# An SSD branch projection as seven block products, with the sums of its weights made early and the gates kept as tanh

## The chip, the cores and the metric

One Trainium2 chip, one NeuronCore of it. The metric is device time in microseconds (us) for one execution of the kernel; where several runs are given, the median counts. A core has TensorE (PE, matmuls; PEld is its weight load), VectorE (DVE), ScalarE (ACT), GpSimd (POOL) and SyncE (SP, which issues the DMAs), each with an instruction queue of its own that it works through in order.

## The reference

One layer on 1024 tokens of width 1024 in float32: a mixer with two branches, attention (A) and a Mamba-2 state space branch (B, "SSD"), then a gated feed-forward part. The part that matters here is how the branches are merged:

```python
D_MODEL, SEQ, D_INNER = 1024, 1024, 2048
h = rmsnorm(x, pre_norm_mix) * (1.0 + scale_m) + shift_m
q_lat, kv_lat, k_idx, w_idx, z, xbc, dt_raw, g_a, g_b = jnp.split(h @ w_in, IN_SPLITS, axis=-1)
y_a = sparse_mla_attention(...) @ w_o_attn
y_b = ssd_mixer(...) @ w_o_ssd          # rmsnorm(y * silu(z), ssd_norm), 1024 x 2048, times 2048 x 1024
mix = (jax.nn.sigmoid(g_a) * y_a + jax.nn.sigmoid(g_b) * y_b) @ w_out
x = x + gate_m * rmsnorm(mix, post_norm_mix)
h2 = rmsnorm(x, pre_norm_ffn) * (1.0 + scale_f) + shift_f
u_gate, u_up = jnp.split(h2 @ w_ffn_in, 2, axis=-1)
x = x + gate_f * rmsnorm((jax.nn.silu(u_gate) * u_up) @ w_ffn_out, post_norm_ffn)
```

## The kernel before

Activations are held transposed, features on the 128 partitions and tokens along the free dimension, in two halves b = 0, 1 of 512 tokens (`half(b)`). A float32 product is made of three matmuls: both operands are split into a rounded high part and the remainder, and hi x hi, lo x hi and hi x lo are added up in PSUM. One matmul is 128 x 128 weights by 128 x 512 activations. So a product over 16 k-tiles takes 48 matmuls for each tile of 128 outputs and each half.

Weights come as a stream, `W` (class `Stream`, L135): for each 4 k-tiles SP loads `wraw` (256 KB), ACT rounds it to `whi` (L153), POOL subtracts to get `wlo` (L154). The load, the rounding and the subtraction of a tile are issued up to two tiles ahead of the tile in use. Since every queue is in order, `whi` and `wlo` stand behind whatever ACT and POOL were given before. Tile buffers come from arenas: EV for short-lived tiles of 512 columns, `H_`, `Q` and `R` for operands. PSUM has three banks "d" (`bank_d`) and five general ones (`bank`), which the norms use too. A scheduler orders the engines' instructions, except that in the stages marked `in_order` TensorE keeps the order of the code.

The stages that the change touches, in order of time:

- Input projection with the convolved tiles (`conv_group`, L1018) and the gate tiles (`gate`, L970): `conv_group(0)` and `conv_group(1)` come among the first; from group 2 on each tile is followed by one unit of `weight_sums` (L1004), which adds blocks of w_ffn_out on POOL and stores the sums for the feed-forward part, which is computed by seven block products already. Gate a is stored raw in `d_sga`, gate b in `d_gb`.
- The SSD loop, with `beside()` as filler between its steps: the rest of gate b (`gate_run`), the attention branch times w_o_attn (`poa_run`, L1272: a `poa` product, emptied by a DVE copy, stored in `d_ya`), and the first y tiles (`y_load`, L1226: load from `d_y`, ACT scales and rounds to `yh`, DVE makes the remainder `yw` with one scalar_tensor_tensor). The loop writes y, already gated by silu(z), to `d_y`, and sums its squares in `ysq`.
- `merge(b)` (L1362), for each of 8 output tiles: loads of gate b, `d_ya` and gate a, two Sigmoids on ACT, gate a times y_a on DVE, the `pos` product of 48 matmuls over all of y, then `mrg` = pos times the norm `rys`, times gate b (POOL), plus the other branch, and its two parts `mg`.
- `mixed(b)` (L1399): the `pot` product with w_out, 24 matmuls for each of 8 tiles, and the sum of squares for the norm.
- `residual_steps(b)` (L1427): norm, residual, second norm. `ffn_input(b)` (L1453) makes the input of the feed-forward part.

The order is merge(0), mixed(0), merge(1) with the residual of half 0 among its first tiles, mixed(1), and then the early feed-forward products with the residual of half 1 among them. A norm is `rstd` (matmuls into `p`, `v` on DVE at L265, `r` on POOL at L267) and `rspread` (transposes into `prn`, L273).

## Time and profile before

| what | value |
|---|---|
| runs | 2365.05, 2358.47, 2360.74 us; median 2360.74 |
| profiled execution | span 2362.1 us, no other time of it is listed |
| granted TensorE clock, mean | 0.993 of full speed |
| products and norms from the first `pos` (1435.0 us) to the first feed-forward product (1707.7 us) | 272.7 us |
| `whi` on ACT, `wlo` on POOL, mean of one | 627 ns, 1392 ns |
| table loads on ACT at the Sigmoid of `merge` (L1370) | 1, of 1.28 us |

How to read it: the page gives, for each engine, the time in which it was busy and the groups of instructions that cost most, each with its line, its operands, its count, its busy time, the mean duration of one and the idle time before it with what ended it. The timeline lists single instructions by start and duration in us; the windows give the same busy times for stretches of the span. A matmul's duration runs from its start to the modelled end of its pipeline, so that consecutive matmuls overlap.

### The profile page before, as it was taken

The page shows a single profiled execution, that of the slowest core. Times are in us where ns is not written, and L with a number is a line of the kernel's source. Part 1 is how long each engine was busy: PE and PEld are TensorE (multiplying, and loading weights), DVE is VectorE, ACT ScalarE, POOL GpSimd, SP SyncE. Part 2 cuts the span into 40 slices and gives each one's busy share as a digit, 9 for nine tenths or more (in the row PEclk, how much of TensorE's full clock was granted, in tenths as well). Part 3 has the DMA queues.
Part 4 walks back from the last instruction along what each step waited for, and adds up shares of the span by engine and source line. Part 5 has one row for each costly group of instructions (what it writes and reads, how often), then busy time and mean ns, then how long its engine had stood idle before and what let it go on. Part 6 is the DMA issues. An engine that isn't in the chain of part 4 may idle for free. (4 is left out here: it accounts for less than half of the span.)

```text
span 2362.1 us, 35006 instructions
## 1 busy us (share of the span) xinstructions
PE 2326.5 (98%) x11832; PEld 1907.8 (81%) x11832; DVE 1578.2 (67%) x2994; ACT 1217.9 (52%) x2361; POOL 1168.5 (49%) x911
## 2 busy tenths in 40 slices
PE   8999999999999999999999999999999999999997
PEld 5878888888888888888887787888888788888886
DVE  5467887599676777666677875346476766645775
ACT  4346666576545555555676664454545222235542
POOL 1445552522244555552445455556768545554556
PEclk9999999999999999999999999999999999999999
DMA  7137542623222323334678766566474444428665
GB/s 270 63 134 238 193 169 94 196 90 101 96 81 85 99 90 101 95 94 150 217 245 282 240 220 227 184 209 197 126 265 134 142 152 154 159 95 280 210 190 171
DMA packets 237891, 386.10 MB, mean 163 GB/s; under 512 B 24032, under 2 KB 91792, under 8 KB 237712
## 3 DMA queue, kind: packets, MB, share of 16 engines
q1 hardware_dynamic: 224464, 362.31, 47.1%
q10 hardware_dynamic: 13248, 21.56, 3.1%
q8 instruction: 93, 1.52, 0.3%
q14 instruction: 86, 0.70, 0.1%
HBM read 288.07 MB, written 98.85 MB: 164 GB/s over the span
## 5 line engine op out<-in xcount | busy, mean ns | idle before, releaser
L154 POOL TENSOR_TENSOR wlo<-wraw,whi 128x512 fp32r<-128x512 f32 x246 | 341.7, 1392 | 420.6 <-ACT whi L153 381.4
L1533 PE MATMUL p<-xh,wr 128*128 128x512 f32 x880 | 273.1, 391 | 2.4 <-DVE g L1623 2.4
L153 ACT ACTIVATE whi<-wraw 128x512 fp32r<-128x512 f32 x246 | 153.7, 627 | 207.5 <-issue 58.8
L1527 POOL TENSOR_TENSOR wr<-a,wr 128x512 fp32r<-128x512 f32 x107 | 151.1, 1426 | 95.3 <-ACT wr L1526 63.2
L1533 PEld LDWEIGHTS p<-xh,wr 128*128 128x128 f32 x880 | 166.0, 189 | 37.3 <-DVE g L1623 2.8
L1533 PE MATMUL p<-xl,wr 128*128 128x512 f32 x440 | 171.8, 390 | 0.0
L249 POOL TENSOR_TENSOR fwl<-fw,fwh 128x512 fp32r<-128x512 f32 (+1 forms) x78 | 108.8, 1406 | 102.3 <-ACT fwh L248 38.7
L323 POOL TENSOR_TENSOR adaw<-adaw,cs 128x512 f32<-128x512 f32 x64 | 68.3, 1067 | 156.3 <-DMA adaw<-ada_w 128.0
L853 ACT ACTIVATE lg<-lg,mx 128x256 f32<-128x256 f32 (+7 forms) x128 | 99.0, 774 | 56.5 <-DVE mx L850 56.2
L1526 ACT ACTIVATE wr<-a 128x512 fp32r<-128x512 f32 x107 | 65.9, 629 | 108.4 <-PE p L1533 80.9
L648 DVE SCALAR_TENSOR_TENSOR acc<-rel,widx,acc 128x384 f32<-128x384 f32 (+2 forms) x90 | 104.9, 1190 | 15.4 <-ACT rel L643 15.2
L1533 PE MATMUL p<-h2h,wr 128*128 128x512 f32 x352 | 110.2, 391 | 1.0 <-ACT xh L248 1.0
L698 ACT ACTIVATE junk<-acc,cand__2215 128x1024 bf16<-128x1024 f32 (+2 forms) x96 | 86.2, 898 | 39.4 <-DVE cand__2215 L741 30.6
L228 PE MATMUL pos<-yh,wlo 128*128 128x512 f32 x256 | 101.4, 396 | 1.0 <-POOL wlo L154 1.0
L228 PE MATMUL pos<-yh,whi 128*128 128x512 f32 x256 | 100.7, 393 | 1.3 <-ACT whi L153 1.3
L643 ACT ACTIVATE rel<-prel 128x512 f32<-128x512 f32 (+3 forms) x160 | 77.0, 523 | 46.8 <-PE prel L642 43.3
L228 PE MATMUL pos<-yw,whi 128*128 128x512 f32 x256 | 100.7, 393 | 0.0
L1533 PEld LDWEIGHTS p<-xl,wr 128*128 128x128 f32 x440 | 82.9, 188 | 17.3
L1527 POOL TENSOR_TENSOR wr<-s,wr 128x512 fp32r<-128x512 f32 x44 | 61.7, 1407 | 65.1 <-ACT wr L1526 58.7
L696 DVE TENSOR_SCALAR_CACHE_REDUCE junk<-acc,cand__2224 128x896 bf16<-128x896 f32 (+2 forms) x96 | 88.5, 922 | 1.5
L850 DVE CUSTOM_DVE_ANT_0 lg<-plg,nm 128x256 f32<-128x256 f32 (+1 forms) x128 | 51.5, 403 | 53.0 <-PE plg L841 52.3
L874 PE MATMUL pt<-ident,lg 128*128 128x128 f32 x576 | 82.3, 272 | 0.0
(671 smaller groups left out, 7301.5 us busy)
## 6 DMA issues: line engine op xcount, KB each, us to landing
wraw<-w_in SPq DMA_DIRECT2D x129, 256.0 KB, 2.9
a<-w_ffn_in SPq DMA_DIRECT2D x122, 256.0 KB, 3.3
al<-d_a SPq DMA_DIRECT2D x88, 256.0 KB, 4.5
adaw<-ada_w SPq DMA_DIRECT2D x64, 256.0 KB, 2.9
al<-d_ac SPq DMA_DIRECT2D x32, 512.0 KB, 5.1
wraw<-w_o_ssd SPq DMA_DIRECT2D x64, 256.0 KB, 3.1
d_a<-g SPq DMA_DIRECT2D x42, 256.0 KB, 2.2
ada<-ada_p SPq DMA_DIRECT2D x16, 512.0 KB, 7.8
```

The source lines that it names most:

```text
L153: self.hi = behind(S.activation(hi[:, :kt], raw[:, :kt], AF.Copy))
L154: self.lo = behind(G.tensor_tensor(lo[:, :kt], raw[:, :kt], f(hi[:, :kt]), op=OP.subtract))
L228: T.matmul(o, wt[:, k0 + i, :], xs[k][xi][b][:, sl], start=pi == 0 and i == 0 and wt is hi and xi == 0, stop=pi == len(pcs) - 1 and i == l ...
L249: (lo_eng or V).tensor_tensor(lo, src, f(hi), op=OP.subtract)
L643: S.activation(rel[:, 512 * b:512 * b + w_], pr[:, 0:w_], AF.Relu)
L648: V.scalar_tensor_tensor(acc[i][:, 0:n], rel[:, 0:n], ws, acc[i][:, 0:n], op0=OP.mult, op1=OP.add)
L696: V.tensor_scalar(jk, y, a_, 0.0, op0=op, op1=OP.add, accum_out=o)
L698: S.activation(jk, y, AF.Sign, scale=-1.0, bias=a_, accum_out=o)
L853: S.activation(lg[:, 0:n], lg[:, 0:n], AF.Exp, scale=-1.0, bias=m, accum_out=rr[:, 2 * t + hh:2 * t + hh + 1])
L874: T.transpose(ptv[:, hh, t, :], PR[hh, t][:, j * P:(j + 1) * P], ident)
L1527: G.tensor_tensor(w[:, 1], src, f(w[:, 0]), op=OP.subtract)
L1533: T.matmul(p, w[:, wi, i], X[x][i][xi], start=start and i == 0 and k == 0, stop=i == 3 and k == 2, skip_group_check=True)
```

## The change

The projection by w_o_ssd is cut into blocks: the two halves of the tokens, the first and the last 8 of its 16 k-tiles (SK = 8), and the first and the last four of its 8 output tiles. Seven products of such blocks, each over 8 k-tiles for 4 output tiles c, take the place of the eight that two halves, two k-blocks and two output blocks make. A step (i, c) of `ssd_step` is one product i for one tile c, 24 matmuls; products add up in the same PSUM bank or are added from SBUF. Operands: product 1 is the first 8 k-tiles of half 0 with the weights as they are, 2 the last 8 of half 0; 3, 5, 6 and 7 have sums of y tiles (`last_sum`, `both_sums`, `third_sum`), 4 the last 8 k-tiles of half 1. The weights of 4 to 7 are sums of blocks, from `d_s`. The order is `SEQ` (22 steps), mixed(0), `SEQ1` (6 steps, with the residual of half 0 between them), mixed(1). Each step first gives ACT, DVE and POOL its `tasks`: sums and splits for later steps, and gates; their loads are issued one step before.

The sums of the weights are made by `ssd_sums`, in eight units on POOL with buffers and code like those of `weight_sums`, after the last two tiles of `conv_group(0)`, the four of `conv_group(1)` and the first two z gates. Gates are stored as tanh(x/2), so that a sigmoid is (tanh + 1)/2; the two halves are taken together as a scale of 0.5 where `mix` leaves PSUM. Gate a is multiplied in `poa_run`, with `d_sga` loaded into `ya` there; gate b with the norm in `merge_gate`. The Sigmoids go. Half of the `xr` additions of half 0 move to POOL.

```diff
-    def gate(c, dst, fn):
+    def gate(c, dst, fn, scale=1.0):
         p = wide(c)
         for b in BS:
             t = EV("g")
-            S.activation(t, p[b], fn)
+            S.activation(t, p[b], fn, scale=scale)
...
+    s_units = iter([(c, k0) for c in range(4) for k0 in (0, 4)])
+    def ssd_sums(c, k0):
+        b11, b12, b21, b22 = sum_bufs
+        for x, t, o in ((b11, c, 0), (b12, 4 + c, 0), (b22, 4 + c, SK), (b21, c, SK)):
+            tc.add_manual_dep(SP.dma_start(x, a["w_o_ssd"][t][:, o + k0:o + k0 + 4]).ins, W.issue, mybir.DependencyInfo(
+                mybir.DependencyClass.NoSync, mybir.DependencyReason.DATA), reason="behind")
+        G.tensor_tensor(b11, b12, b11, op=OP.subtract)
+        G.tensor_tensor(b12, b22, b12, op=OP.subtract)
+        G.tensor_tensor(b22, b11, b22, op=OP.subtract)
+        G.tensor_tensor(b21, b21, b22, op=OP.add)
+        for i, x in enumerate((b11, b22, b12, b21)):
+            SP.dma_start(d_s[i, c][:, k0:k0 + 4], x)
     def conv_group(g):
-        for t in group_tiles(g):
+        for i, t in enumerate(group_tiles(g)):
             conv_out(conv(*t))
             if g > 1:
                 weight_sums(*next(units))
+            elif g or i > 1:
+                ssd_sums(*next(s_units))
...
+    def y_raw(k, b):
+        t = EV("yl")
+        SP.dma_start(t, d_y[k][:, half(b)])
+        return t
+    def y_parts(i, j, src, where, scale=None, eng=V):
+        hi, lo = where("yh", dt=F32R), where("yw", dt=F32R)
+        if scale is None:
+            ins = S.activation(hi, src, AF.Copy)
+            eng.tensor_tensor(lo, src, f(hi), op=OP.subtract)
+        else:
+            ins = S.activation(hi, src, AF.Copy, scale=scale)
+            V.scalar_tensor_tensor(lo, src, scale, f(hi), op0=OP.mult, op1=OP.subtract)
+        YO[i][j] = hi, lo
+        return ins.ins
+    def y_load(ks, places):
         for k in ks:
-            t = EV("yl")
-            SP.dma_start(t, d_y[k][:, half(b)])
-            where = places(k)
-            yh, yw = where("yh", dt=F32R), where("yw", dt=F32R)
-            j = S.activation(yh, t, AF.Copy, scale=col("ssd_norm", k))
-            if b == 0 and k > 11:
-                tc.add_manual_dep(j.ins, W.hi, mybir.DependencyInfo(
-                    mybir.DependencyClass.NoSync, mybir.DependencyReason.DATA), reason="behind")
-            V.scalar_tensor_tensor(yw, t, col("ssd_norm", k), f(yh), op0=OP.mult, op1=OP.subtract)
-            YB[b][k] = ([yh] * 2, [yw] * 2)
+            y_parts(1 + k // SK, k % SK, y_raw(k, 0), places(k), col("ssd_norm", k))
...
         def poa_run(t, b, w):
             ya = EV("ya")
+            SP.dma_start(ya, d_sga[t][:, half(b)])
             p = bank_d("poa")
             yield from dense_steps(p, b, w, AT)
-            if t:
-                V.tensor_copy(ya, p)
-            else:
-                anchor(S.activation(ya, p, AF.Copy))
+            i = V.scalar_tensor_tensor(ya, ya, 1.0, p, op0=OP.add, op1=OP.mult)
             SP.dma_start(d_ya[t][:, half(b)], ya)
...
-            S.activation(sb, sb, AF.Sigmoid)
-            S.activation(ga, ga, AF.Sigmoid)
-            V.tensor_tensor(ld, ld, ga, op=OP.mult)
-            p = bank_d("pos")
-            pcs = wpieces(list(range(16))) if t or b else [(first_w, 0, ks8[:4])] + wpieces(list(range(4, 16)))
-            dense([(p, b, ALL)], pcs, YB[b])
...
+    def merge_in(t, b):
+        sb, ld = EV("sgb"), EV("yal")
+        for x, src in ((sb, d_gb), (ld, d_ya)):
+            SP.dma_start(x, src[t][:, half(b)])
+        return sb, ld
+    def merge_gate(b, sb):
+        V.scalar_tensor_tensor(sb, sb, 1.0, rys[b], op0=OP.add, op1=OP.mult)
+    def merge_out(t, b, src, sb, ld, eng=V):
+        V.tensor_tensor(sb, src, sb, op=OP.mult)
+        eng.tensor_tensor(sb, sb, ld, op=OP.add)
+        hi, lo = in_r("mg")
+        i1 = S.activation(hi, sb, AF.Copy).ins
+        i2 = V.tensor_tensor(lo, sb, f(hi), op=OP.subtract).ins
+        MG[b][t] = ([hi] * 2, [lo] * 2)
...
-            (G if b and t % 2 == 0 else V).tensor_tensor(xr, mix[t], xr, op=OP.add)
+            (G if t % 2 == 0 else V).tensor_tensor(xr, mix[t], xr, op=OP.add)
...
+    SRC = {1: [ws_[c][:, 0:SK] for c in range(4)], 2: [ws_[c][:, SK:16] for c in range(4)],
+           3: [ws_[4 + c][:, SK:16] for c in range(4)], 4: d_s[3], 5: d_s[0], 6: d_s[1], 7: d_s[2]}
+    SEQ = [(i, c) for i in (1, 2, 6, 5, 3) for c in range(4)] + [(7, 0), (7, 1)]
+    SEQ1 = [(4, 0), (7, 2), (4, 1), (7, 3), (4, 2), (4, 3)]
+    for seq in (SEQ, None, SEQ1, None):
+        for x in seq or range(8):
+            W.plan(col_tile(SRC[x[0]][x[1]] if seq else a["w_out"][x]))
...
+    def both_sums(k):
+        def work(x):
+            y21, y22 = x[:2]
+            S.activation(y21, y21, AF.Copy, scale=col("ssd_norm", k))
+            V.scalar_tensor_tensor(y21, y22, col("ssd_norm", SK + k), y21, op0=OP.mult, op1=OP.add)
+            if k % 2 == 0:
+                S2.append(R("s2", (P, 2, 512)))
+            s2 = S2[-1][:, k % 2]
+            if k < 4:
+                hi, lo = YO[1][k]
+                V.tensor_tensor(s2, f(hi), y21, op=OP.subtract)
+                V.tensor_tensor(s2, f(lo), s2, op=OP.add)
+            else:
+                V.scalar_tensor_tensor(s2, x[2], col("ssd_norm", k), y21, op0=OP.mult, op1=OP.subtract)
+            y_parts(6, k, s2, Q)
+            y_parts(5, k, y21, H_, eng=G)
+        return lambda: [y_raw(k, 1), y_raw(SK + k, 1)] + [y_raw(k, 0)] * (k > 3), work
+    def last_sum(k):
+        def work(x):
+            s2 = S2[k // 2][:, k % 2]
+            V.scalar_tensor_tensor(s2, x[0], col("ssd_norm", SK + k), s2, op0=OP.mult, op1=OP.add)
+            y_parts(3, k, s2, H_, eng=(V, G)[k % 2])
+        return lambda: (y_raw(SK + k, 0),), work
+    def third_sum(k, where):
+        def work(x):
+            (G if k % 2 else V).tensor_tensor(x[0], x[0], x[1], op=OP.subtract)
+            y_parts(7, k, x[0], where, col("ssd_norm", k))
+        return lambda: (y_raw(k, 0), y_raw(k, 1)), work
...
+    tasks = {}
+    for c in range(4):
+        tasks[1, c] = [both_sums(c), plain(2, 4 + c, 0)]
+        tasks[2, c] = [both_sums(4 + c)]
+        tasks[6, c] = [last_sum(2 * c), last_sum(2 * c + 1)] + [merge_first(c // 2)] * (c % 2)
+        tasks[5, c] = [third_sum(k, Q) for k in ((0, 1), (2,), (3,), (4,))[c]] + [merge_first(2 + c // 2)] * (c % 2)
+        tasks[3, c] = [third_sum(5 + c, H_)] * (c < 3) + [gates_of(4 + c, 0)]
+        tasks[7, c] = [gates_of(4 + c, 1)]
+        tasks[4, c] = [gates_of(c, 1)]
+    plains = iter([plain(4, k, 1) for k in range(SK)])
+    loaded = {}
+    def ahead_of(x):
+        if x in tasks and x not in loaded:
+            loaded[x] = [load() for load, _ in tasks[x]]
+    def ssd_step(x, nxt):
+        i, c = x
+        ahead_of(x)
+        for (_, work), got in zip(tasks[x], loaded[x]):
+            work(got)
+        if nxt:
+            ahead_of(nxt)
+        w = [first_w if x == (1, 0) else W.next(), W.next()]
+        start = i in (1, 2, 7)
+        if start:
+            banks[{1: 0, 2: 1, 7: 2}[i], c] = (bank_d if i == 2 else bank)("pos")
+        p = banks[{2: 1, 7: 2, 4: 2}.get(i, 0), c]
+        for k in range(SK):
+            for n, (wi, xi) in enumerate(P3):
+                T.matmul(p, w[k // 4][wi][:, k % 4], YO[i][k][xi], start=start and k == 0 and n == 0,
+                         stop=k == SK - 1 and n == 2, skip_group_check=True)
+        if i == 1:
+            S.activation(p1s[c], p, AF.Copy)
+        elif i == 2:
+            V.tensor_tensor(p1s[c], p, p1s[c], op=OP.add)
+        elif i == 6:
+            S.activation(u2s[c], p, AF.Copy)
+        elif i == 5:
+            u4s.append(Q("u4"))
+            S.activation(u4s[c], p, AF.Copy)
+        elif i == 3:
+            merge_out(4 + c, 0, p, *gates[4 + c, 0], eng=G)
+        elif i == 7:
+            V.tensor_tensor(u4s[c], p, u4s[c], op=OP.add)
+            merge_out(4 + c, 1, u4s[c], *gates[4 + c, 1], eng=G)
+        else:
+            V.tensor_tensor(u2s[c], p, u2s[c], op=OP.add)
+            merge_out(c, 1, u2s[c], *gates[c, 1])
+    def ry(b):
+        rys[b] = wp.tile([P, 4, P], F32, name="rys", tag=("uraw", "uh")[b], bufs=1).rearrange("p k m -> p (k m)")
+        r = rstd([ysq[b]], D_INNER)
+        yield
+        S.activation(rys[b], rspread(r), AF.Copy)
+        yield
+    x1, y1 = [], []
+    with in_order(mybir.EngineType.PE):
+        norm = [ry(0), ry(1)]
+        for n, x in enumerate(SEQ):
+            ssd_step(x, (SEQ + SEQ1)[n + 1])
+            if n < 4:
+                next(norm[n // 2])
...
+        out = []
+        for t, _ in enumerate(mixed(0, MG[0], out)):
+            load, work = next(plains)
+            work(load())
+        rest = residual_steps(0, *out, x1, 2)
+        for n, x in enumerate(SEQ1):
+            ssd_step(x, (SEQ1 + [None])[n + 1])
+            if n < 4:
+                next(rest)
+        out = []
+        for t, _ in enumerate(mixed(1, MG[1], out)):
+            if t in (0, 2, 3):
+                next(rest)
+            if t == 3:
+                x1 = ffn_input(0, x1)
```

In `mixed(0)`, each tile is followed by one `plain(4, k, 1)`: a load, ACT's rounding and DVE's remainder of a y tile of half 1 for product 4.

What this moves on the engines is seen at three places. POOL, from the first weights of the input projection (`wlo`, `ul`) to the second norm (`r`); `adaw` and `vt` are here the buffers in which the blocks of w_o_ssd are added. Before:

```order
L154 TENSOR_TENSOR wlo<-wraw,whi 128x512 x2
L170 TENSOR_TENSOR ul<-uraw,uh 128x512
L154 TENSOR_TENSOR wlo<-wraw,whi 128x512 x4
L267 TENSOR_TENSOR r<-v,nhalf 128x4
L154 TENSOR_TENSOR wlo<-wraw,whi 128x512
```

And of the change:

```order
L172 TENSOR_TENSOR ul<-uraw,uh 128x512
L156 TENSOR_TENSOR wlo<-wraw,whi 128x512 x2
L1029 TENSOR_TENSOR adaw<-adaw 128x512
L156 TENSOR_TENSOR wlo<-wraw,whi 128x512
L1030 TENSOR_TENSOR adaw<-vt,adaw 128x512
L1031 TENSOR_TENSOR vt<-adaw,vt 128x512
L156 TENSOR_TENSOR wlo<-wraw,whi 128x512
L1032 TENSOR_TENSOR vt<-vt 128x512
L270 TENSOR_TENSOR r<-v,nhalf 128x4
```

One unit of four additions now stands between the same four `wlo` and ahead of `r`. The second place is ACT around the end of the SSD loop (`ysqt<-zy` is its last square) and the first steps of the products. Before:

```order
L153 ACTIVATE whi<-wraw 128x512
L1208 ACTIVATE ysqt<-zy 128x512
L153 ACTIVATE whi<-wraw 128x512 x2
L1232 ACTIVATE yh<-yl,vec 128x512
L153 ACTIVATE whi<-wraw 128x512
L1232 ACTIVATE yh<-yl,vec 128x512 x3
L153 ACTIVATE whi<-wraw 128x512
L1370 ACT_TABLE_LOAD
L1370 ACTIVATE sgb<-sgb 128x512
```

And of the change (`s` are the sums of y tiles, L1542 scales a y tile of half 1):

```order
L1542 ACTIVATE yl<-yl,vec 128x512
L155 ACTIVATE whi<-wraw 128x512
L1230 ACTIVATE ysqt<-zy 128x512
L1257 ACTIVATE yh<-s_14946 128x512 x2
L155 ACTIVATE whi<-wraw 128x512
L1257 ACTIVATE yh<-yl 128x512
L1260 ACTIVATE yh<-yl,vec 128x512
L1542 ACTIVATE yl<-yl,vec 128x512
L1257 ACTIVATE yh<-yl 128x512
L155 ACTIVATE whi<-wraw 128x512
```

Behind the last square `whi` used to stand behind y tiles that were loaded; now it stands behind tiles that DVE adds up first (`s`, and `yl` after L1543). The third place is DVE at the same time. Before, from the last `zy` to the first norm (`v`):

```order
L1202 SCALAR_TENSOR_TENSOR zy<-ld,dsk,zy 128x256 x2
L1236 SCALAR_TENSOR_TENSOR yw<-yl,vec,yh 128x512
L1277 COPY ya<-poa 128x512
L1236 SCALAR_TENSOR_TENSOR yw<-yl,vec,yh 128x512 x5
L1277 COPY ya<-poa 128x512
L1236 SCALAR_TENSOR_TENSOR yw<-yl,vec,yh 128x512
L1215 TENSOR_TENSOR ysq<-ysq,ysqt 128x256 x2
L265 TENSOR_SCALAR v<-p_14914 128x4
```

And the beginning of the same stretch in the change:

```order
L1224 SCALAR_TENSOR_TENSOR zy<-ld,dsk,zy 128x256 x2
L1549 TENSOR_TENSOR s_14946<-yh,yl 128x512
L1307 SCALAR_TENSOR_TENSOR ya<-ya,poa 128x512
L1550 TENSOR_TENSOR s_14946<-yw,s_14946 128x512
L1543 SCALAR_TENSOR_TENSOR yl<-yl,vec 128x512
L1549 TENSOR_TENSOR s_14946<-yh,yl 128x512
L1237 TENSOR_TENSOR ysq<-ysq,ysqt 128x256
L1550 TENSOR_TENSOR s_14946<-yw,s_14946 128x512
L1258 TENSOR_TENSOR yw<-s_14946,yh 128x512
L1237 TENSOR_TENSOR ysq<-ysq,ysqt 128x256
```

Where 11 instructions stood between `zy` and `v`, 24 stand now: the `yw` of the first operands come earlier, and the sums of the first steps take their place.

More of the change, by code (lines that the diff above doesn't have):

```diff
@@ L1399, in mixed @@
-    def mixed(b, MG):
-        mix, sacc = [], None
-        for t in range(8):
-            W.plan(col_tile(a["w_out"][t]))
-        two = []
+                T.matmul(o, wt[:, k % 4, :], xs[k][xi][0], start=first and n == 0 and i == 0,
+                         stop=last and n == len(ks) - 1 and i == 2)
+    def mixed(b, MG, out):
+        mix, sacc, two = [], None, []
         for t in range(8):
@@ L1648, in build @@
     with in_order(mybir.EngineType.PE):
[L1649 to L1651 removed]
+        fill, rest = early(range(EARLY)), residual_steps(1, *out, y1)
         for n in (2, 1, 9, 4):
```

138 lines of the change are left out of this document (66 added, 72 removed).

## The prediction

> **What bounds the kernel now.** I read the page's busy shares first, then the groups of TensorE by line, then single rows.
>
> ```profile
> span 2362.1 us, 35006 instructions
> PE 2326.5 (98%) x11832; PEld 1907.8 (81%) x11832; DVE 1578.2 (67%) x2994; ACT 1217.9 (52%) x2361; POOL 1168.5 (49%) x911
> L228 PE MATMUL pos<-yh,wlo 128*128 128x512 f32 x256 | 101.4, 396 | 1.0 <-POOL wlo L154 1.0
> L228 PE MATMUL pos<-yh,whi 128*128 128x512 f32 x256 | 100.7, 393 | 1.3 <-ACT whi L153 1.3
> L228 PE MATMUL pos<-yw,whi 128*128 128x512 f32 x256 | 100.7, 393 | 0.0
> ```
>
> TensorE is busy in 98% of the span, all else in 67% or less, so a matmul that goes is time that goes, if the others keep up. The three `pos` groups are the product that the change rewrites: 768 matmuls, 302.8 us of busy time, hardly any idle time ahead of them. But matmuls overlap, so 393 ns is how long one is under way and not what it costs. The cost is the distance between starts, which the timeline of TensorE shows.
>
> ```profile
> 1654.70 0.39 PE L228 MATMUL pos<-yw,whi 128*128 128x512 f32 x1
> ...
> 1663.99 0.39 PE L1397 MATMUL pot<-mg,whi 128*128 128x512 f32 x1
> ```
>
> From the first of these rows to the last, 41 matmuls start, evenly: 9.29 / 41 = **0.227 us** each. A row of 24 (one step of the new order) takes 5.45 us. Next, the table of windows: for each stretch the busy time of PE, PEld, DVE, ACT, POOL (with instructions), the granted clock, the DMA share and GB/s.
>
> ```profile
> 1435.00:1528.00 93.00, 91.04 (x400) 74.24 (x399) 29.04 (x41) 36.93 (x62) 55.03 (x42) 0.98 0.55 179
> 1592.70:1620.20 27.50, 26.29 (x119) 21.20 (x119) 27.42 (x32) 12.91 (x24) 16.04 (x11) 1.00 0.64 210
> 1418.00:1438.60 20.60, 20.60 (x96) 17.16 (x95) 17.58 (x23) 11.84 (x19) 9.77 (x7) 1.00 0.81 291
> 80.00:120.00 40.00, 40.00 (x189) 33.19 (x188) 14.03 (x27) 14.31 (x23) 12.95 (x11) 1.00 0.23 73
> 160.00:200.00 40.00, 38.65 (x180) 31.16 (x179) 27.09 (x46) 22.60 (x37) 22.11 (x18) 1.00 0.75 256
> 320.00:360.00 40.00, 39.41 (x186) 32.83 (x185) 32.57 (x45) 24.53 (x47) 21.81 (x14) 1.00 0.47 162
> 1283.00:1293.00 10.00, 7.61 (x21) 4.68 (x20) 7.64 (x8) 7.68 (x16) 6.41 (x5) 0.67 0.94 313
> ```
>
> The first row is `merge(0)`: DVE is busy 29 of 93 us, so there is room for work beside the products. The second is the residual of half 0, where DVE is full; the third the end of the SSD loop, where DVE is already busy 17.6 of 20.6 us.
>
> **The change part by part.**
>
> *Fewer matmuls.* Before: 2 halves x 8 tiles x 16 k x 3 = 768. After: 7 products x 4 tiles x 8 k x 3 = 672. The 96 that go are on the path: 96 x 0.227 = **-21.8 us**. `pot` and the norms keep their numbers.
>
> *The start of the products.* Before, TensorE stalls there. Its rows and ACT's:
>
> ```profile
> 1443.28 0.40 PE L228 MATMUL pos<-yh,wlo 128*128 128x512 f32 x1
> 1445.00 0.51 PE L228 MATMUL pos<-yh,whi 128*128 128x512 f32 x1 [1.32 <-ACT whi L153]
> 1446.41 0.50 PE L228 MATMUL pos<-yh,wlo 128*128 128x512 f32 x1 [0.64 <-POOL wlo L154]
> ...
> 1447.56 0.63 PE L228 MATMUL pos<-yh,wlo 128*128 128x512 f32 x1
> 1447.98 0.63 PE L228 MATMUL pos<-yh,whi 128*128 128x512 f32 x1
> ...
> 1450.65 0.39 PE L228 MATMUL pos<-yh,whi 128*128 128x512 f32 x1
> 1443.71 0.72 ACT L1232 ACTIVATE yh<-yl,vec 128x512 fp32r<-128x512 f32 x1 [8.02 <-DMA yl<-d_y]
> 1447.54 1.28 ACT L1370 ACT_TABLE_LOAD   x1
> ```
>
> From 1443.28 to 1450.65 only 13 `pos` matmuls start (2.95 us at the cadence), so about **4 us** are lost, in part by idle time, in part because starts are 0.42 us apart around 1447.56. ACT stood 8 us at a load of `d_y`, and the weights' `whi` stood behind it; then came the table load. After, the table load goes, and the first step needs only the y tiles loaded inside the SSD loop. But the first input sums need the second half of y, which the last chunk writes, and `whi` stands behind those `yl` and `yh` of ACT in the same way; ACT's copies in turn wait for DVE, which has 24 instructions between its last `zy` and the first norm's `v`. Bounds: the stall goes (-4) or doubles and a bit (+6). I take **+1**, near the stall that is there, since the same kind of wait takes its place. A further wait: of the five general PSUM banks the four accumulators of the first steps hold four, so the fourth of them needs the bank of the first norm's `prn`, which ACT empties behind its copies. It is inside the +6.
>
> *The input sums during the products.* Each step works one step ahead: in the first four steps five DVE instructions with two SBUF operands each, and on POOL two `wlo` and one subtraction. What such work costs side by side is seen just before, in DVE's and POOL's timeline:
>
> ```profile
> 1429.61 6.94 DVE L1236 SCALAR_TENSOR_TENSOR yw<-yl,vec,yh 128x512 fp32r<-128x512 f32 x5
> 1437.08 0.73 DVE L1236 SCALAR_TENSOR_TENSOR yw<-yl,vec,yh 128x512 fp32r<-128x512 f32 x1
> 1427.31 1.78 DVE L1236 SCALAR_TENSOR_TENSOR yw<-yl,vec,yh 128x512 fp32r<-128x512 f32 x1
> 1430.85 5.16 POOL L154 TENSOR_TENSOR wlo<-wraw,whi 128x512 fp32r<-128x512 f32 x3 [0.60 <-ACT whi L153]
> 1439.75 1.29 POOL L154 TENSOR_TENSOR wlo<-wraw,whi 128x512 fp32r<-128x512 f32 x1
> ```
>
> Alone a `yw` takes 0.73 us and a `wlo` 1.29; beside each other up to 1.78, and 5.16 / 3 = 1.72. Five and three of them took 6.94 us, a step has 5.45: each of the first four steps puts DVE 1.5 us behind, 6 us by the fourth. The work is needed one to four steps later (the `5` and `6` products come after four steps of `2`, which have three such instructions each), so most of this is absorbed. From the first sum to the last `mg` that `mixed(0)` needs there are about 105 DVE instructions over 22 steps = 120 us and some 15 us before them: 1.29 us each would still fit, and the row of groups below says about 1.0. Bounds 0 (all absorbed) to +13 (the second rival); I take **+2**, nearer to the 29 of 93 us of the window.
>
> [...]
>
> *The sums of the weights.* Eight units of four POOL additions with four loads and four stores of 256 KB each, beside the first convolved tiles. The existing sums of w_ffn_out (L1011 to L1014, 12 units from 163.6 to 346.8 us) are the same work:
>
> ```profile
> L1011 POOL TENSOR_TENSOR adaw<-adaw 128x512 f32<-128x512 f32 (+1 forms) x12 | 14.8, 1234 | 38.3 <-DMA adaw<-w_ffn_out 24.8 <-DMA vt<-w_ffn_out 7.8 <-PE prel L642 5.7
> POOL adaw L1011 <- DMA adaw<-w_ffn_out: 24.8, 8, 8.2
> 95.20 1.01 POOL L267 TENSOR_TENSOR r<-v,nhalf 128x4 f32<-128x4 f32 x1 [1.47 <-DVE v L265]
> 100.59 0.60 PE L273 MATMUL prn<-ident,r 128*128 128x128 f32 x4
> ```
>
> (The second row is one of POOL's waits: in all, times, longest.) POOL waits for the loads 24.8 us in 8 waits, and what stands behind it is `wlo` for TensorE; still PE is idle only 1.35 us in 160 to 200 and 0.59 in 320 to 360. For 8 units in place of 12 that is about **+1**. New is that POOL's `r` of the norms, done at 96.2 and used at 100.59, now also stands behind such additions, in a stretch where POOL is busy 12.95 of 40 us and DMA 0.23. Four additions are about 5 us (4 x 1.29), close to the 4.4 us between. Bounds 0 to +5.
>
> *Gates as tanh, `d_sga` loaded at w_o_attn.* 32 Sigmoids and 16 DVE products leave the merge, a step off the path there. The DVE copy that empties `poa` becomes an instruction that also reads `ya`, and 16 loads of 256 KB move into the SSD loop. There DMA is already 0.94 busy in 1283 to 1293 us, where PE loses time at a granted clock of 0.67. The work ahead of that stall is as it was, so I keep it. Bounds 0 to +4, I take **+1**.
>
> [...]
>
> *The end.* `residual_steps(0)` now runs between the six last steps, two tiles at a time.
>
> ```profile
> L1437 DVE TENSOR_TENSOR xr<-mix,xr 128x512 f32<-128x512 f32 x8 | 7.7, 1020 | 0.0
> L1380 DVE TENSOR_TENSOR mrg<-pos,rys 128x512 f32<-128x512 f32 x7 | 4.8, 692 | 18.0 <-PE pos L228 17.7 <-ACT rys L1378 0.3
> 1616.78 0.39 PE L228 MATMUL pos<-yw,whi 128*128 128x512 f32 x1
> 1618.07 1.02 PE L262 MATMUL p<-ones,mix 128*128 128x1 f32 x8 [0.90 <-DVE mix L1441]
> ```
>
> Before, in 1592.7 to 1620.2, DVE's full stretch held up the second norm by 0.9 us, and a `wlo` shortly ahead of it by 0.3. After, half of the `xr` additions go to POOL, but the last merges stand in the same queue: about 37 instructions at 0.7 to 1.0 us, 26 to 37 us, where 6 steps less the norm give about 28. Bounds -1.5 to +6; I take **0**.
>
> *Sum.* -21.8 + 1 + 2 + 1 + 1 + 0 = -16.8 us. It is made against the profiled execution, of which the span, 2362.1 us, is all that is listed; it lies 1.4 us over the median of the runs, 2360.74, and inside their range. 2362.1 - 16.8 = 2345.3; less the 1.4, **2344 us**.
>
> **The rivals.**
>
> 1. *The old stalls go and none comes.* -21.8 - 4 - 1.5 = -27.3: 2333.4 us. For it: DVE's 29 of 93 us. Against: ACT's queue still puts `whi` behind sums that wait for the last chunk. Chance 0.13.
>
> 2. *POOL and DVE can't keep the step.* If two of them beside each other always took 1.77 us, and one alone 0.7 or 1.3, the steps of kind 1, 2, 6, 5 and 3 would need 6.7, 5.3, 6.7, 5.9 and 6.0 us by the instructions in the code: 122.4 us for twenty steps, against 109. 13.4 us come back with the +3 of the other terms less what is counted for this: -21.8 + 13.4 + 3 = -5.4, so 2355 us. [...] Chance 0.15.
>
> 3. *Slower: DVE becomes the bound of the products.* If each of the 85 or so instructions with two SBUF operands pays 1.77 us, whatever POOL does, and the other 20 pay 0.69, DVE needs 164 us where 135 are there: 29.5 - 21.8 = +8, so 2369 us. It decides from a mean of (135 + 21.8) / 105 = 1.5 us an instruction; the full stretch 1592.7 to 1620.2 has 27.42 / 32 = 0.86. Chance 0.06.
>
> 4. *The sums of the weights hold up the early products.* POOL's longest wait for a load was 8.2 us, and the weights are about one step, 5.45, ahead: 2.8 us in each of 8 units, 22 us, and the gain is gone: 2344 - 1 + 22 = 2365 us. Against it: the windows of 12 such units. Chance 0.05.
>
> 5. *A matmul saves its duration.* 96 x 0.393 = 37.7 instead of 21.8: 2328 us. The even starts at 0.227 speak against it. Chance 0.03.
>
> The forecast, 2338 to 2350, has the remaining 0.58. That the change leaves the matmuls is excluded by the order of the instructions.
>
> **How the numbers follow.** The predicted time is the forecast's. The range takes in rival 1 at 2333.4 and most of rival 2: **2333 to 2357**. Outside are 0.06 + 0.05 + 0.03 and a part of rival 2. 0.3% is 7.1 us, about what a measurement of this kernel can tell from no change: faster means under 2353.6. That is the forecast, rivals 1 and 5, and the better half of rival 2: 0.58 + 0.13 + 0.03 + 0.07 = 0.81. Rival 2's other half and most of rival 4 are within 0.3%: 0.12. Slower: 0.07.
>
> **What would show it.** The `pos` groups of the new code hold 672 matmuls, and their starts in a quiet step are 0.227 us apart (rival 5). Waits of PE for `whi`, `wlo` or `yh` in the first eight steps of some 4 to 7 us together show the middle terms; over 12 us with DVE and POOL both full, rival 2; DVE full through all twenty steps, rival 3. PE idle beyond 3 us in 80 to 200 us shows rival 4. The window around 1283 to 1293 us stays as it is, or the term for `d_sga` was too small. No table load between the last chunk and the first merge. What would make the prediction wrong most easily is a wait in the first steps that drops the clock, or stalls of before that vanish altogether.

## The result, and the profile after

The changed kernel takes 2385.79 us (median of 4 runs, 2381.24 to 2388.66) against 2361.46 us (4 runs): a ratio of 1.01, with a 95% interval of 1.0083 to 1.0116. It is **slower by 1%**, where 0.7% faster was forecast. The profiled execution of the change took 2381.24 us, with a span of 2379.5 us.

The matmuls are gone, as the page shows in its busy time and the groups of the new `pos`:

```profile
PE 2317.4 (97%) x11736; PEld 1893.8 (80%) x11736; DVE 1650.6 (69%) x3040; ACT 1217.8 (51%) x2362; POOL 1233.2 (52%) x947
L1625 PE MATMUL pos<-yh,wlo 128*128 128x512 f32 x224 | 90.2, 403 | 8.7 <-POOL wlo L156 8.6
L1625 PE MATMUL pos<-yh,whi 128*128 128x512 f32 x224 | 90.1, 402 | 1.4 <-ACT whi L155 1.0
L1625 PE MATMUL pos<-yw,whi 128*128 128x512 f32 x224 | 89.1, 398 | 0.0
```

There are 672 in place of 768. What is new stands behind the bar: TensorE waits 8.6 us for `wlo` there, where it waited 1.0.

To see where the time came from, take the start of the first TensorE row of each stage in both traces and subtract. In us:

| kernel | to first input product | input projection, to the dt sums | gates, attention, to first `poa` | SSD loop, to first `pos` | products, to first FFN product | rest, to TensorE's last row |
|---|---|---|---|---|---|---|
| before | 74.7 | 98.5 | 1102.4 | 159.5 | 272.5 | 645.7 |
| change | 72.3 | 106.5 | 1103.6 | 164.7 | 274.7 | 648.8 |
| difference | -2.4 | **+8.0** | +1.2 | **+5.3** | **+2.2** (forecast: -18.8) | +3.1 |

The sum is +17.4, the difference of the two spans. The medians are 24.3 us apart: the profiled execution of the change is 4.6 us faster than its median, and the rest of the gap is on the side of the kernel before. So 6.9 us of the result stand in no stage of this pair. The first and third columns hold code that the change hardly touches; in the kernels below they lie between 72.0 and 75.5 and between 1102.8 and 1106.5 (79 in the first where units of sums were moved ahead), so a difference of 2 to 4 us in one stage of one trace says little.

The products split further: 22 steps of `SEQ`, 119.9 us at 0.227 us a matmul, took 142.6; the last six, 32.7 at the cadence, 36.1; `mixed(1)`, 43.5 before, 52.5. In the windows of the change (columns as before) the first row holds the first 83 us of the products:

```profile
1447.00:1530.00 83.00, 70.64 (x289) 55.10 (x290) 79.21 (x69) 38.49 (x71) 64.57 (x41) 0.94 0.78 255
1530.00:1590.00 60.00, 60.00 (x266) 49.67 (x266) 21.33 (x22) 23.01 (x39) 36.63 (x28) 1.00 0.53 176
160.00:200.00 40.00, 34.91 (x152) 27.79 (x151) 25.51 (x48) 19.41 (x30) 22.59 (x18) 0.91 0.66 232
```

DVE is busy 79.2 of 83 us and then only 21.3 of 60: over the whole stage it has room, as the prediction reckoned, but not in the first eleven steps. There TensorE is idle 12.4 us, and by an estimate from the same row its granted clock of 0.94 costs another 5 us (0.06 of 83); from 1530 us on it runs without a pause, at the cadence. How the lack reaches TensorE is seen in the timelines of POOL, DVE and PE:

```profile
1448.42 3.43 POOL L1258 TENSOR_TENSOR yw<-yl,yh 128x512 fp32r<-128x512 f32 x2
1451.82 1.71 POOL L156 TENSOR_TENSOR wlo<-wraw,whi 128x512 fp32r<-128x512 f32 x1
1448.93 1.78 DVE L1261 SCALAR_TENSOR_TENSOR yw<-yl,vec,yh 128x512 fp32r<-128x512 f32 x1
1450.63 1.77 DVE L1543 SCALAR_TENSOR_TENSOR yl<-yl,vec 128x512 f32<-128x512 f32 x1
1453.59 0.50 PE L1625 MATMUL pos<-yh,wlo 128*128 128x512 f32 x1 [2.05 <-POOL wlo L156]
1454.84 0.63 PE L1625 MATMUL pos<-yh,whi 128*128 128x512 f32 x1
1455.27 0.63 PE L1625 MATMUL pos<-yw,whi 128*128 128x512 f32 x1
1467.59 0.77 PE L276 MATMUL prn<-ident,r 128*128 128x128 f32 x4 [3.51 <-POOL r L270]
```

POOL's two remainders take 1.72 us each beside DVE's 1.77 and stand ahead of a `wlo`; TensorE waits 2.05 us, and some matmuls later its starts are 0.43 us apart: its granted clock is 0.50 in 1454.4 to 1457.4 us. The norm's `r` waits for `v`, which stands in DVE's full queue (it runs at 1465.92, behind 24 others since the last `zy`): 3.5 us more.

In `mixed(1)`, ACT's and PE's rows show the same in another place:

```profile
1674.43 0.63 ACT L1406 ACTIVATE mg<-sgb 128x512 fp32r<-128x512 f32 x1 [5.16 <-DVE sgb L1404]
1678.30 0.63 ACT L1406 ACTIVATE mg<-sgb 128x512 fp32r<-128x512 f32 x1 [2.72 <-DVE sgb L1404]
1678.84 0.61 ACT L155 ACTIVATE whi<-wraw 128x512 fp32r<-128x512 f32 x1
1679.50 1.14 PE L1416 MATMUL pot<-mg,whi 128*128 128x512 f32 x2 [2.92 <-ACT whi L155]
```

A weight tile is rounded only after two `mg` that wait for DVE. And in the input projection, in the timelines of PE, DVE and POOL, with three rows of before behind them:

```profile
169.33 0.79 PE L231 MATMUL pw<-h0h,whi 128*128 128x512 f32 x1 [5.09 <-DVE cv L988]
158.64 1.40 DVE L557 TENSOR_TENSOR dt_tmp<-dt_tmp 128x256 f32<-128x256 f32 x1
158.25 1.52 POOL L1032 TENSOR_TENSOR vt<-vt 128x512 f32<-128x512 f32 x1
164.54 0.21 DVE L988 SCALAR_TENSOR_TENSOR cv<-pw,vec,cv 128x1 f32<-128x1 f32 x1
...
166.01 0.50 PE L228 MATMUL pw<-h0h,whi 128*128 128x512 f32 x1 [1.35 <-DVE cv L985]
156.67 0.42 DVE L554 TENSOR_TENSOR dt_tmp<-dt_tmp 128x256 f32<-128x256 f32 x1
161.75 0.21 DVE L985 SCALAR_TENSOR_TENSOR cv<-pw,vec,cv 128x1 f32<-128x1 f32 x1
```

A small DVE instruction of the dt chain takes 1.40 us beside the last addition of a unit of weight sums (0.42 before), the convolution's first tap behind that chain is done 2.8 us later than before, and TensorE waits 5.1 us for the bank (1.35 before, at the same tile). That row is only the end of the delay, though: the chain's reciprocal already starts 2.4 us later than before (156.41 against 153.99), behind a DVE wait of 1.89 us for ACT's `cv`. In the window from 160 to 200 us above, TensorE is busy 34.9 us (38.65 before), at a clock of 0.91.

### The profile page after: what moved, and what is told of

The parts are those of the page before. It is cut to its first block, busy times and chain, and to the rows that moved or that the text cites. A ratio compares the mean times of both kernels' runs of the same rounds, so it can differ in the third digit from the quotient of the medians.

```text
span 2379.5 us, 35122 instructions
## 1 busy us (share of the span) xinstructions
PE 2317.4 (97%) x11736; PEld 1893.8 (80%) x11736; DVE 1650.6 (69%) x3040; ACT 1217.8 (51%) x2362; POOL 1233.2 (52%) x947
## 5 line engine op out<-in xcount | busy, mean ns | idle before, releaser
L156 POOL TENSOR_TENSOR wlo<-wraw,whi 128x512 fp32r<-128x512 f32 x238 | 332.3, 1399 | 371.4 <-ACT whi L155 340.8
L155 ACT ACTIVATE whi<-wraw 128x512 fp32r<-128x512 f32 x238 | 148.7, 627 | 211.8 <-issue 52.5
L701 ACT ACTIVATE junk<-acc,cand__2216 128x1024 bf16<-128x1024 f32 (+2 forms) x96 | 86.3, 898 | 39.5 <-DVE cand__2216 L744 31.2
L1625 PE MATMUL pos<-yh,wlo 128*128 128x512 f32 x224 | 90.2, 403 | 8.7 <-POOL wlo L156 8.6
L1625 PE MATMUL pos<-yh,whi 128*128 128x512 f32 x224 | 90.1, 402 | 1.4 <-ACT whi L155 1.0
L1625 PE MATMUL pos<-yw,whi 128*128 128x512 f32 x224 | 89.1, 398 | 0.0
L853 DVE CUSTOM_DVE_ANT_0 lg<-plg,nm 128x256 f32<-128x256 f32 (+1 forms) x128 | 51.5, 404 | 52.9 <-PE plg L844 52.3
L1416 PE MATMUL pot<-mg,whi 128*128 128x512 f32 x256 | 80.6, 396 | 3.6 <-ACT whi L155 3.4
```

Of the source, the lines that this page charges most:

```text
L155: self.hi = behind(S.activation(hi[:, :kt], raw[:, :kt], AF.Copy))
L156: self.lo = behind(G.tensor_tensor(lo[:, :kt], raw[:, :kt], f(hi[:, :kt]), op=OP.subtract))
L701: S.activation(jk, y, AF.Sign, scale=-1.0, bias=a_, accum_out=o)
L1416: T.matmul(o, wt[:, k % 4, :], xs[k][xi][0], start=first and n == 0 and i == 0, stop=last and n == len(ks) - 1 and i == 2)
L1625: T.matmul(p, w[k // 4][wi][:, k % 4], YO[i][k][xi], start=start and k == 0 and n == 0, stop=k == SK - 1 and n == 2, skip_group_check=True)
```

## The experiments

Time is compared as a ratio to the kernel before on the same chip, where it took 2363.9 to 2367.0 us; stages are compared between traces, as above. All stages, in us, in the order of the columns above, with the parts of the products:

| kernel | input projection | SSD loop | 22 steps | last six | `mixed(1)` | products in all | rest |
|---|---|---|---|---|---|---|---|
| before | 98.5 | 159.5 | | | 43.5 | 272.5 | 645.7 |
| change | 106.5 | 164.7 | 142.6 | 36.1 | 52.5 | 274.7 | 648.8 |
| e1 no weight sums | 98.1 | 166.0 | 142.6 | 37.6 | 54.2 | 278.0 | 649.2 |
| e2 plain operands | 106.1 | 167.5 | 128.6 | 36.3 | 51.5 | 259.9 | 649.2 |
| e3 sums on DVE | 106.3 | 167.6 | 137.8 | 37.9 | 48.8 | 268.0 | 648.6 |
| e4 gates alone | 98.3 | 162.9 | | | 44.9 | 267.6 | 646.3 |
| e5 even, on DVE | 100.8 | 167.6 | 138.1 | 39.4 | 46.7 | 267.7 | 648.0 |
| e6 even, POOL kept | 103.7 | 166.4 | 150.0 | 37.6 | 53.1 | 284.1 | 647.3 |
| e7 gates in merge | 98.1 | 159.0 | | | 44.8 | 275.8 | 645.3 |
| e8 residual later | 100.1 | 163.7 | 139.3 | 38.4 | 49.3 | 270.5 | 656.3 |
| e9 whi first | 108.6 | 162.8 | 140.7 | 37.6 | 51.4 | 273.2 | 654.7 |
| e10 even, whi first | 102.5 | 163.8 | 126.5 | 39.5 | 46.9 | 256.5 | 650.6 |
| e12 places, last six | 103.0 | 163.5 | 129.1 | 36.3 | 51.2 | 260.2 | 651.1 |
| e13 loop order | 100.2 | 159.8 | 129.1 | 36.5 | 52.0 | 261.2 | 652.7 |
| e14 loop and whi | 99.6 | 161.9 | 128.7 | 40.8 | 45.5 | 258.5 | 648.4 |
| e15 FFN as before | 102.9 | 162.2 | 129.2 | 39.5 | 46.9 | 259.2 | 653.6 |

**The sums of the weights.**

```diff
-            elif g or i > 1:
-                ssd_sums(*next(s_units))
...
-           3: [ws_[4 + c][:, SK:16] for c in range(4)], 4: d_s[3], 5: d_s[0], 6: d_s[1], 7: d_s[2]}
+           3: [ws_[4 + c][:, SK:16] for c in range(4)], 4: [ws_[4 + c][:, 0:SK] for c in range(4)],
```

> The changed kernel without the early sums of weights: products 4 to 7 read unsummed tiles of w_o_ssd instead (the output is left wrong in the second half of the tokens and in half of the output tiles). Theory: the sums cost 8.0 us between 75 and 175 us (in the changed kernel's trace TensorE's distance to the kernel before goes from -2.4 to +5.6 us there, by a 5.1 us wait for DVE's cv, two waits for r and a halved clock), so about 2378 us against 2386. Rival: the sums are nearly free as the twelve units of w_ffn_out were (1.3 us), and the early loss comes from the order of DVE's dt chain: 2384 us or more, with the wait for cv still in the trace.

2379.77 us, ratio 1.0062 (1.0045 to 1.0078). The input projection takes 98.1 us, as before: all 8 us were the sums, and the wait for `cv` that the rival kept is gone. e5 and e6 below move units from the last tiles of conv group 1 to z gates: with the last one moved the stage takes 103.7, with the last two 100.8 (102.5 in e10, at the same places). So what a unit costs depends on where it stands, and the units beside the dt chain were the dear ones. By which way they cost is not separated: by the longer DVE instruction beside POOL's (1.40 us above, 0.42 before), by POOL's `r` behind four additions, or by the order on DVE.

**The gates.** e4 is the kernel before with the gates' part of the change alone; e7 the same with both gates multiplied in `merge`.

```diff
         def poa_run(t, b, w):
             ya = EV("ya")
+            SP.dma_start(ya, d_sga[t][:, half(b)])
...
+            V.scalar_tensor_tensor(ya, ya, 1.0, p, op0=OP.add, op1=OP.mult)
```

> The kernel before with only the gates' part of the change: tanh of half stored, d_sga loaded and multiplied in poa_run, no Sigmoids, 0.5 at mix. Theory (the d_sga loads and the DVE product at w_o_attn are what moved the SSD loop back by 4.3 us): about +4 in the loop and -4 at the start of the merge, where the table load goes: 2361 us, within 3. Rival 1: a gain in the merge and no loss in the loop, 2357 us. Rival 2: the loop's loss comes from the order of the y loads, not from the gates: the loop as before.

> The kernel before with gates stored as tanh of half, no Sigmoids and no table load, but both gates multiplied in the merge on DVE and nothing changed at w_o_attn. Theory (e4's +3.4 us in the SSD loop come from d_sga and the product in poa_run, its -4.9 us between the first pos and the feed-forward part from the Sigmoids that are gone): the loop as before, the products about 268 us in place of 272.5, in all 4 to 5 us less than before, 2360 against 2364.5. Rival (the gain of e4 is from the 16 DVE products that left the merge): the products stay at 271 us or more, the time as before.

e4: ratio 0.9999 (0.9988 to 1.0009): the SSD loop loses 3.4 us, the products gain 4.9. The loop's part is seen in the waits of TensorE in e4 (in all, times, longest); before, it waited 1.3 us for `al` and never for `cbm`:

```profile
PE pyd L1185 <- DVE al L1145: 4.1, 5, 1.1
PE pcb L1140 <- DVE cbm L1143: 2.2, 1, 2.2
```

e7: ratio 1.0013 (1.0 to 1.0025). The loop is as before, as the theory said, but the products take 275.8 us, so the rest of it falls: the gain in e4 is not the Sigmoids and the table load that went, since e7 has neither. What e4 has beyond e7 in the merge is 16 DVE products and 16 loads less; no run tells these two apart. Both the 3.4 and the 4.9 us are also little more than single traces differ by.

**Too much work or the wrong engine?** e2 leaves out the sums of y tiles; e3 has all the remainders and sums on DVE.

```diff
-            y_parts(5, k, y21, H_, eng=G)
+            y_parts(5, k, y21, H_)
...
-            y_parts(3, k, s2, H_, eng=(V, G)[k % 2])
+            y_parts(3, k, s2, H_)
```

> The changed kernel without the sums of y tiles: products 3, 5, 6 and 7 take plain y tiles (output wrong), some 20 instructions of DVE and 16 of POOL fewer in the products' stage; all matmuls, weights and loads but four are as they were. Theory (DVE and POOL cannot keep the pace in the first eleven steps, 1447 to 1530 us, where DVE is busy 79 of 83 us): the stage from the first pos to the first feed-forward product goes from 274.7 to about 253 us, the time to about 2365 us. Rival (the weights' loads are late, with the DMA queues 0.85 busy in 1447 to 1475 us, or the banks): the waits for wlo stay, 2382 us or more.

> The changed kernel with all the sums and remainders that POOL makes in the products' stage put on DVE; POOL has only wlo and the norms' r there. The same arithmetic. Theory of the queue (wlo stands behind POOL's yw, which wait for DVE and ACT): the 8.6 us of waits for wlo go, and with them some 5 us of halved clock: about 2374 us. Theory of throughput (DVE itself is full until 1530 us, whatever POOL does): DVE gets some 20 instructions more, 15 us at 0.7 each, the waits move to whi, to the norm's r and to the merges: 2386 to 2400 us.

e2: ratio 1.003 (1.002 to 1.0039); the 22 steps fall from 142.6 to 128.6 us, so the sums account for 14 us of the 22.7 above the cadence. The rival of late weights falls with it. The products stay 7 us above the 253 expected: `mixed(1)` keeps its 51.5. And **even without the sums the kernel is slower than before**, by what the other stages lost.

e3: ratio 1.0067 (1.0049 to 1.0085), in the middle between its two theories, and that is told by the window of its first eleven steps (in the change these take 82.7 us and fill the first window above):

```profile
1450.90:1527.10 76.20, 68.18 (x288) 53.59 (x289) 71.17 (x83) 38.42 (x69) 39.37 (x26) 0.96 0.84 271
```

For the same steps DVE has 83 instructions in place of 69 and is busy 71.2 us in place of 79.2: 0.86 us each, against 1.15. POOL has 26 in place of 41, and its busy time falls by 25.2 us. With part of the work on POOL, DVE was busy longer than with all of it: 15 of POOL's instructions fewer, and DVE's busy time in these steps became 8 us shorter.

**When the work is given out.**

```diff
-        tasks[6, c] = [last_sum(2 * c), last_sum(2 * c + 1)] + [merge_first(c // 2)] * (c % 2)
+        tasks[6, c] = [merge_first(c // 2)] * (c % 2)
...
-            if n < 4:
-                next(norm[n // 2])
+            if n in (0, 2, 3, 5):
+                next(norm[n // 3])
```

> The changed kernel with POOL's sums and remainders on DVE (as in e3), the y sums given out more evenly (last_sum with the steps of product 5 in place of 6, third_sum with those of 3), the first four sums from a fresh load (one DVE instruction fewer each), the two norms of y spread over steps 0, 2, 3 and 5, and the units of weight sums after two tiles of conv group 0, two of group 1 and four z gates. Theory (DVE is full only in the first eleven steps, since its work is given out too early, and the early loss is the one unit that meets DVE's dt chain): from the first pos to the first feed-forward product 258 us (268.1 in e3, 274.7 in the changed kernel), from 75 to 175 us some 2 us more than before in place of 8.0; in all 2365 us. Rival: the products stay above 266 us since waits move to the merges at the end; then 2373 us.

> The changed kernel with POOL's sums kept on POOL, the y sums given out as in e5 (but the first four as in the change), the norms spread as in e5, and the units after two tiles of conv group 0, three of group 1 and three z gates. Theory of the place in time (what counts is when DVE gets the work): products 262 us. Theory of the shared time of DVE and POOL (each of POOL's subtractions slows one of DVE's by 1 us): products 268 us or more, clearly behind e5. Early part: 75 to 175 us some 2 us over before if only the last unit of conv group 1 did harm, 5 us or more if every unit does.

One run each: e5 2373.25 us, e6 2387.91, before 2366.95 on that chip. Giving the sums out later changes nothing in e5's 22 steps (138.1 against 137.8 in e3) and makes e6's worse (150.0 against 142.6). So my theory of the place in time falls; with POOL's part on POOL much the same plan is 12 us slower than in e5. The waits for the norm's `r` are gone in both, and the steps are no shorter for it: that wait was a symptom. The window of e5's first eleven steps shows what is left:

```profile
1446.80:1522.80 76.00, 68.60 (x289) 51.77 (x288) 63.32 (x76) 37.10 (x66) 39.36 (x26) 0.98 0.82 268
```

DVE is busy 63.3 of 76.0 us, 8 less than in e3, and the steps take as long: here it is no longer the amount of DVE's work that sets the pace.

**The end of the stage.**

```diff
-            if n < 4:
+            if n < 2:
                 next(rest)
...
-            if t == 3:
+            if t == 4:
```

> As e5, but of the residual of half 0 only the norm and the first two tiles run between the six last steps, the rest beside mixed(1) and ffn_input two pot tiles later. Theory (mixed(1) took 52.5 us in the changed kernel against 43.5 before, since DVE has the last merges and the residual at once and whi stands behind mg on ACT): six last steps and mixed(1) together from 86.1 us in e5 to about 79. Rival (the waits at mixed(1) come from the merges alone): 85 us or more, and the feed-forward part starts late.

2378.69 us; the last six steps and `mixed(1)` together 87.7 us against 86.1 in e5. The rival's number holds: doing the residual later does not help `mixed(1)`, and ffn_input now comes too late (one wait of 4.6 us for `h2l`, the rest 656.3 us).

**The order on ACT.** e9 is the change with two weight tiles called before a step's tasks, and ACT's roundings of sums behind the newest `whi`; e10 is e5 with the same.

```diff
+        w = [first_w if x == (1, 0) else W.next(), W.next()]
         for (_, work), got in zip(tasks[x], loaded[x]):
             work(got)
...
+            ins = behind_whi(S.activation(hi, src, AF.Copy))
```

> The changed kernel with one thing more: each step calls for its two weight tiles before its tasks, and ACT's roundings of y sums and of mg, and its scaled copies, are ordered behind the newest whi. No instruction more or fewer. Theory (DVE's lag alone would do no harm, as its sums are needed four steps later; it reaches TensorE because whi stands in ACT's queue behind roundings that wait for DVE): the 22 first steps take 128 us or less (142.6 in the changed kernel, 119.9 at the cadence), the time about 2372 us against 2386. Rival (the sums themselves are late, or wlo stands behind POOL's yw): 138 us or more.

> e5 with the order of e9, and in mixed(1) the weights of w_out loaded with their second half first, so that the last merged k-tiles meet the last weight tile and no other is held for them. Theory: the 22 steps 126 us or less (138.1 in e5), the last six steps and mixed(1) 80 us or less (86.1 in e5), the time about 2362 us, no slower than before on this chip. Rival: as in e9, the steps stay at 135 us or more; then 2370 us.

e9, 2386.46 us, in its first 51 us and then in PE's timeline:

```profile
1447.00:1498.00 51.00, 50.09 (x233) 41.26 (x232) 45.51 (x42) 27.55 (x48) 39.34 (x25) 1.00 0.79 253
1502.90 0.49 PE L1630 MATMUL pos<-yh,whi 128*128 128x512 f32 x1 [3.06 <-ACT yh L1262]
1507.62 0.80 PE L1630 MATMUL pos<-yw,whi 128*128 128x512 f32 x1 [4.23 <-DVE yw L1263]
1534.44 0.79 PE L1630 MATMUL pos<-yh,wlo 128*128 128x512 f32 x1 [4.61 <-POOL wlo L156]
```

For 51 us TensorE hardly waits, and then it meets operands that are not there yet. The order only moved the lag: 140.7 us, the rival's number. In e10, where DVE gets through its work, the same order gives 126.5 us (138.1 without it), and the window of the first fourteen steps has DVE busy 61.8 of 82.7 us with 74 instructions. The DMA queues are as busy as in the change (0.78), so they are not what held the change's steps up:

```profile
1447.30:1530.00 82.70, 81.23 (x369) 66.82 (x368) 61.80 (x74) 42.25 (x74) 44.02 (x30) 1.00 0.78 258
```

The products take 256.5 us, 16 less than before, and the kernel 2365.39 us (one run; before 2363.89). The turned weights of w_out did not help: 86.4 us for the end, against 80 expected.

**The loop and the last six steps.** e12 is e10 with the units after all four tiles of group 0 and the last six steps in another order; e13 is e12 with ACT's first `yh` behind the loop's exponentials.

```diff
+            i = y_parts(1 + k // SK, k % SK, y_raw(k, 0), places(k), col("ssd_norm", k))
+            for j in exps[0]:
+                tc.add_manual_dep(i, j, mybir.DependencyInfo(
...
-    SEQ1 = [(4, 0), (7, 2), (4, 1), (7, 3), (4, 2), (4, 3)]
+    SEQ1 = [(7, 2), (4, 0), (7, 3), (4, 1), (4, 2), (4, 3)]
```

> e10 with two more moves: the units of weight sums after all four tiles of conv group 0 and the first four z gates (none in group 1), and the six last steps in the order (7,2), (4,0), (7,3), (4,1), (4,2), (4,3), so that product 4 of a tile comes no sooner than two steps after DVE reads product 7 from the same bank. Theory: 75 to 175 us 1 us over before or less (4.0 in e10), the wait of 3.3 us for DVE's u gone, six last steps and mixed(1) 82 us (86.4 in e10); about 2358 us, 5 less than before. Rival: every unit costs where it stands, 4 us again, and DVE is late at the end in any order.

> e12 with ACT's rounding of the first y tiles ordered behind the last exponentials of the SSD loop. Theory (the loop's loss of 4 to 8 us is ACT's yh, which wait for their load ahead of the exponentials that al needs): from the first poa to the first pos 160 us as before (163.8 in e10); in all 4 us less than e12. Rival (the loss is DVE's product in poa_run, as e4 says, which had 3.4 us without any new y sums): 163 us or more, the same as e12.

e12 is a miss, 2372.42 us: the wait for `u` goes (last six 36.3, from 39.5), and `mixed(1)` gets it back (51.2, from 46.9); with units beside the first tiles, the first input product starts at 79 us instead of 72 to 75. e13, 2368.54: the SSD loop takes 159.8 us, as before, 3.7 less than e12. The `yh` of ACT that wait for a load stood ahead of the exponentials that `al` needs; TensorE's waits for `al` fall from 6.2 to 3.6 us. With the same order the loop takes 161.9 us in e14 and 162.2 in e15, against 163.8 in e10, so the gain is 2 to 4 us and near what single traces differ by.

**All mends together.**

```diff
         for t in range(8):
+            if n == 8:
+                x_load(t)
             xr = xs[t]
```

> e10 with the one move of e13 that held: ACT's rounding of the first y tiles behind the SSD loop's exponentials (places of the weight sums and order of the last six steps as in e10). Theory (the losses of the changed kernel are order on ACT and shared time of DVE and POOL, not the block products as such): the loop 160 us as in e13, the products 257 us as in e10, in all 2.5 us less than e10: 2360 to 2363 us on this chip, ratio to before 0.997 to 1.0. Rival (what is taken from one stage comes back in the next, as with e12's last steps): ratio above 1.001.

> e14 without the two small edits behind mixed(1): the order of a FFN product behind the one before (ends), and the early loads of the residual of half 1. Theory (the 3 to 5 us that the feed-forward part has lost in every version of the change come from them): from the first feed-forward product to pfo 424.5 us as before, against 428 to 430 with them, so 3 us less than e14. Rival (the loss comes from DVE's backlog at the end of mixed(1) and the halved clock after it): 428 us or more.

e14: 2364.54 us against 2364.15, ratio 0.9994 (0.9984 to 1.0003): no difference to before, 1% better than the change. The rival's bound is not reached, nor is a gain. e15 (its diff above, with `ends` left out too): 2362.34 us, ratio 0.999 (0.9982 to 0.9999), the one version that is faster than before by more than its interval, by 0.1%; among so many versions, that can be chance. Whether its theory holds stays open. By the traces it falls: the feed-forward part is no shorter (653.6 us against 648.4 in e14). But the trace of e14 is of an execution 5.2 us faster than its median, and that of e15 of one 2.7 us slower, while the medians, from 12 runs each on one chip, are 2.2 us apart in favour of e15, where the theory gave 3. What the feed-forward part loses in most versions of the change, 2 to 9 us, stays open too. It has small waits, most of them early on: 1.15 us for `sqm` and 0.4 for `wr` in e10, neither of them before.

## Why the prediction was wrong

- **96 matmuls at 0.227 us: right.** In 1530 to 1590 us of the change TensorE is busy throughout (60.00 of 60 us, granted clock 1.00), and the 672 are there. The rival of 393 ns each is out.
- **The input sums during the products, +2 (bounds 0 to 13), with the start, +1: this is the step that failed.** "Five and three of them took 6.94 us, a step has 5.45 ... most of this is absorbed" was right in its price and wrong in what followed. The 22 steps took 22.7 us over the cadence, against 6.1 for `merge(0)` (93.3 us for 384 matmuls): +16.6 where +3 was forecast. I spread 105 instructions evenly over 22 steps and 15 us ahead of them, which leaves 1.29 us for each. But the first sum started only 7 us ahead (1440.14, the first `pos` 1447.1), and 69 DVE instructions belong to the first eleven steps, 60 us at the cadence: that leaves 0.87 us for each, and they took 1.15 (rival 2's effect, not rival 3's 1.77). Behind them DVE had hardly any work. And I took a lag of DVE as harmless as long as the sums are needed later: `whi`, `wlo` and `r` stand in the same queues and are needed at once. e3 and e10 show both halves: POOL's share back on DVE -4.8 us, that and the order on ACT -16.1 together, the order alone (e9) -1.9. The -16.1 also holds e5's later sums, which alone changed nothing.
- **The end, 0:** the last six steps lost a little less than `merge(1)` had, but `mixed(1)` lost 9.0 us, which no term held. There `mg` and `whi` share ACT's queue, and DVE is late. With POOL's additions on DVE, `mixed(1)` gets 3.7 (e3) and 5.8 us (e5) back, but the six steps ahead lose 1.8 and 3.3 of it to the wait for `u`; the two together take 88.6 us in the change and 86.1 to 91.8 in every version of it, even without the sums of y tiles (87.8 in e2). Where the rest of this loss comes from is open; moving the residual (e8) did not mend it.
- **The sums of the weights, +1 (bounds 0 to 5):** 8.0, by e1. I took the price of 12 units at another place, and weighed only `r` against the room there. TensorE waited 0.78 us for `r` (to 117.49 us), and 5.1 for the tap behind the dt chain, with a granted clock of 0.50 in 169.9 to 174.2 us, behind that wait; how the units delayed the chain is only in part known (e1). Rival 4 had the price of a late load for TensorE's weights, which isn't what happened.
- **The gates, +1 (bounds 0 to 4):** 5.3 in the loop, of which 3.4 are the gates alone (e4) and about 2 to 4 the order of the first y tiles (e13), each from single traces that differ by as much. The stall that I kept is there as before, 8 us later (granted clock 0.66 in 1291 to 1301 us).
- **The clock:** the sum has no term of its own for it; the prediction names a wait in the first steps that drops the clock as what would make it wrong most easily. In the first steps a granted clock of 0.50 followed the three waits that exceed 2 us (2.05 and 2.04 for `wlo`, 3.51 for `r`), with starts 0.43 us apart for about 3 us. Behind the waits of 1.22 and 1.33 us there it was 1.00 (1487 to 1489.5 and 1518.3 to 1521 us). In all it cost the 5 us estimated above, beside 12.4 of idle time.
- **The sum, by the traces:** -21.8 for the matmuls, +16.6 in the 22 steps, -1.1 in the last six, +9.0 in `mixed(1)`, -0.5 in `mixed(0)`, which is the +2.2 of the products; +8.0, +5.3 and +1.9 in the other stages, 17.4 us in all in place of -16.8.
- The sign was given 0.07; rival 2 was nearest to the loss in the steps, and no rival had all the losses. I took them as independent. Those of the products and, in part, of the input projection have in common the in-order queues and DVE instructions that took longer beside POOL's (a mean of 1.15 us in the first eleven steps, 0.86 in e3), and so they were not independent.
